# Both directions of a chunked state-space core in one masked matrix a head, with dt folded into its rows

## The chip, the cores and the metric

The kernel runs on one core of a Trainium2 chip. The metric is device time in microseconds (us), the median of several executions. Engines are named as the profile names them: PE is TensorE (matmuls), PEld its weight loads, DVE is VectorE, ACT is ScalarE, POOL is GpSimd, SP is SyncE, which here only starts transfers (DMA).

## What is computed

The program is one step through two layers of a hybrid backbone over 128 context and 512 latent tokens: four parallel mixers, a gated sum, an output projection, and an MLP. The change is inside one mixer, the bidirectional state-space mixer (SSD, 8 heads of 64 channels, 2 groups of 64 states, chunks of 128 tokens). Per direction and chunk the reference computes

```
acum = cumsum(dt * (-exp(a_log)))
lmat = exp(where(lower, acum_t - acum_s, -1e30))
xdt = x * dt
scores = einsum('thn,shn->tsh', C, B) * lmat
y_diag = einsum('tsh,shp->thp', scores, xdt)
decay_end = exp(acum_last - acum)
chunk_states = einsum('shn,shp->hpn', B * decay_end, xdt)
y_off = einsum('thn,hpn->thp', C, s_start) * exp(acum)
```

and the mixer's output is `y_f + flip(y_b) + d_skip * x`, where the backward direction runs on flipped inputs. All of this is fp32.

## The kernel before

**Tiling.** Tokens lie in five chunks of 128 (one of context, four of latents). The sequence of the work is a hand-written plan: each mixer is a generator, and a string of letters says which generator advances next (`c` is one chunk of the SSD core, `l` the S5 output product, `g` a gate product, `p`/`P` the projections of the attention). A list scheduler then places the instructions on each engine's queue; each engine works its queue strictly in order. The large products split fp32 weights into a high and a low part: ACT casts the high part (`wh`, L214), DVE or POOL subtracts for the low part (`wl`, L198), and PE multiplies three times (L225, L226, L227). PE works on these products between all the small matmuls of the core.

**The core** is `ssd_core`. It runs once in each layer, over chunks `c`, and inside over two groups `g` of four heads. Matrices have the source token in the partitions and the target token in the columns. For a chunk:

- two PE matmuls of B against C (L1006), and four DVE multiplications by a triangle (L1008) make `cm`, the masked scores, [128, direction, group, 128] (tile `scb`);
- POOL multiplies x by dt for each direction (L1020, recorded at the helper's line L1015): two tiles `sxd`, 128x512;
- for a group, two transfers bring the cumulated decay of the four heads to all partitions (L1029, tiles `sseg`), ACT saves a column (L1030), DVE and POOL subtract (L1031), DVE takes the minimum of the two directions (L1035), ACT exponentiates (L1036). One tile `ee` serves both directions, since each uses its own triangle;
- DVE makes the weights `wd` of the state (L1038), POOL multiplies `ee` by the backward mask into `mf` (L1042), DVE multiplies `ee` by the forward mask (L1043);
- PE makes, for each head, two matmuls into one PSUM region: `ee` by forward `xd` (L1046) and `mf` by backward `xd` (L1047);
- after both groups POOL makes `sxw` twice and `sxD` once (L1048, L1049, recorded at L1015), DVE adds `sxD` to the products in place of x (L1050), PE makes the chunk's states (L1054), ACT copies them out (L1058).

**Buffers.** `scb`, `sxd`, `sxw`, `sxD` and several tiles of other steps share one ring `tx` of 4 buffers; the `sseg` tiles share a ring `td` of 5. A write to a ring's buffer waits until all readers of the tile that held it are done. That orders, for one, POOL's `sxd` of a chunk behind the state matmuls of the chunk before.

## Time and profile before

| what | us |
|---|---|
| median of 3 executions | 3042.03 (3039.22 to 3045.7) |
| the profiled execution | 3031.18 |
| its span, first to last instruction | 3029.4 |
| PE busy | 2841.5 (94%) |
| DVE busy | 1724.3 (57%) |
| ACT busy | 1180.8 (39%) |
| POOL busy | 970.2 (32%) |
| mean granted clock of PE | 0.972 |

Busy is the share of the span in which an engine works on an instruction; waiting instructions are not in it. A granted clock of 1 is 2.4 GHz, 0.5 is 1.2 GHz, the only two levels; a mean between says how long each was held. The core of layer 0 lies between 455 and 575 us of the span, that of layer 1 between 1940 and 2075 us. Everything else in these stretches is products of other steps.

### The profile page before, as it was taken

The page shows a single profiled execution, that of the slowest core. Times are in us where ns is not written, and L with a number is a line of the kernel's source. Part 1 is how long each engine was busy: PE and PEld are TensorE (multiplying, and loading weights), DVE is VectorE, ACT ScalarE, POOL GpSimd, SP SyncE. Part 2 cuts the span into 40 slices and gives each one's busy share as a digit, 9 for nine tenths or more (in the row PEclk, how much of TensorE's full clock was granted, in tenths as well). Part 3 has the DMA queues.
Part 4 walks back from the last instruction along what each step waited for, and adds up shares of the span by engine and source line. Part 5 has one row for each costly group of instructions (what it writes and reads, how often), then busy time and mean ns, then how long its engine had stood idle before and what let it go on. Part 6 is the DMA issues. An engine that isn't in the chain of part 4 may idle for free.

```text
span 3029.4 us, 54102 instructions
## 1 busy us (share of the span) xinstructions
PE 2841.5 (94%) x20782; PEld 2663.8 (88%) x20782; DVE 1724.3 (57%) x3730; ACT 1180.8 (39%) x2660; POOL 970.2 (32%) x1057
## 2 busy tenths in 40 slices
PE   7888898999899999999999889999999999999999
PEld 5888788898689888899998879888898999999999
DVE  7859847765643456646235686475666436433333
ACT  4343463343344242323234536523535434322322
POOL 3737506523212222424111670264131122211111
PEclk9989999999899999999999999999999999999999
DMA  6752253224432735434444323431252323222222
GB/s 238 239 180 90 71 152 111 81 90 134 145 109 72 239 102 174 146 115 154 153 146 132 121 82 111 140 107 58 91 181 86 110 87 112 63 77 74 74 77 84
DMA packets 241858, 364.21 MB, mean 120 GB/s; under 512 B 42272, under 2 KB 104480, under 8 KB 241600
## 3 DMA queue, kind: packets, MB, share of 16 engines
q1 hardware_dynamic: 226848, 336.97, 35.5%
q10 hardware_dynamic: 14752, 23.78, 2.1%
q8 instruction: 164, 2.69, 0.4%
q14 instruction: 94, 0.77, 0.1%
HBM read 294.98 MB, written 65.68 MB: 119 GB/s over the span
## 4 chain that ended last, share of the span: by engine, by line
PE 71%; DVE 15%; issue 4%; DMA 3%; ACT 3%; POOL 2%; SPq 0%; ACTq 0%; DVEq 0%; POOLq 0%
PE dn L225 20%; PE dn L226 19%; PE dn L227 19%; DVE wl L198 2%; DVE B L767 2%; PE mx L290 1%; PE mx L1287 1%; PE pb L1331 1%; PE mx L1461 1%; PE mx L1325 1%; PE mx L1416 1%; DMA sseg<-acum 1%; DVE sc L764 1%; DVE sc L765 1%; PE mx L745 1%
## 5 line engine op out<-in xcount | busy, mean ns | idle before, releaser
L198 POOL TENSOR_TENSOR wl<-wr,wh 128x512 fp32r<-128x512 f32 x207 | 282.6, 1366 | 1271.2 <-ACT wh L214 1151.3
L214 ACT CAST wh<-wr 128x512 fp32r<-128x512 f32 (+1 forms) x614 | 377.4, 620 | 612.9 <-PE dn L226 539.6
L198 DVE TENSOR_TENSOR wl<-wr,wh 128x512 fp32r<-128x512 f32 (+1 forms) x407 | 325.7, 804 | 304.7 <-ACT wh L214 297.3
L225 PE MATMUL dn<-hh,wh 128*128 128x320 f32 x1328 | 422.6, 319 | 8.4 <-ACT us L697 2.7
L227 PE MATMUL dn<-hh,wl 128*128 128x320 f32 x1328 | 420.2, 317 | 3.4 <-DVE wl L198 3.4
L226 PE MATMUL dn<-hl,wh 128*128 128x320 f32 x1328 | 420.1, 316 | 2.8 <-DVE hl L403 1.5
L225 PE MATMUL dn<-nh,wh 128*128 128x320 f32 x992 | 311.7, 315 | 6.6 <-DVE r L1755 6.6
L225 PE MATMUL dn<-fh,wh 128*128 128x320 f32 x1008 | 313.6, 311 | 2.0 <-DVE s5u L595 1.3
L226 PE MATMUL dn<-nl,wh 128*128 128x320 f32 x992 | 308.9, 312 | 3.9 <-DVE nl L403 1.6
L227 PE MATMUL dn<-fh,wl 128*128 128x320 f32 x1008 | 312.0, 310 | 0.0
L226 PE MATMUL dn<-fl,wh 128*128 128x320 f32 x1008 | 311.8, 309 | 0.0
L227 PE MATMUL dn<-nh,wl 128*128 128x320 f32 x992 | 308.0, 311 | 0.0
L226 PE MATMUL dn<-wl,hh 128*128 128x256 f32 (+1 forms) x880 | 258.2, 294 | 16.3 <-DVE wl L198 14.2
L225 PEld LDWEIGHTS dn<-hh,wh 128*128 128x128 f32 x1328 | 254.3, 192 | 16.5 <-issue 3.1
L225 PE MATMUL dn<-wh,hh 128*128 128x256 f32 (+1 forms) x880 | 259.7, 297 | 8.5 <-DVE dtraw L1216 4.2
L227 PEld LDWEIGHTS dn<-hh,wl 128*128 128x128 f32 x1328 | 254.2, 191 | 8.9 <-DVE wl L198 4.6
L226 PEld LDWEIGHTS dn<-hl,wh 128*128 128x128 f32 x1328 | 254.2, 191 | 7.1 <-POOL hl L198 2.1
L227 PE MATMUL dn<-wh,hl 128*128 128x256 f32 (+1 forms) x880 | 257.1, 293 | 0.0
L1547 DVE SCALAR_TENSOR_TENSOR x<-dn,mod,x 128x192 f32<-128x192 f32 (+2 forms) x240 | 98.0, 437 | 225.2 <-PE dn L227 222.2
L225 PE MATMUL dn<-B,wh 128*128 128x320 f32 x640 | 207.8, 326 | 15.1 <-ACT B L834 4.4
L226 PE MATMUL dn<-B,wh 128*128 128x320 f32 x640 | 203.4, 318 | 0.0
L227 PE MATMUL dn<-B,wl 128*128 128x320 f32 x640 | 201.3, 315 | 0.0
(400 smaller groups left out, 6715.0 us busy)
## 6 DMA issues: line engine op xcount, KB each, us to landing
wr<-in_w_fc_dram SPq DMA_DIRECT2D x256, 256.0 KB, 2.8
wa<-in_w_mod_dram SPq DMA_DIRECT2D x160, 256.0 KB, 4.5
wr<-in_w_gate_dram SPq DMA_DIRECT2D x128, 256.0 KB, 2.8
wr<-in_w_tok_dram SPq DMA_DIRECT2D x80, 256.0 KB, 2.9
wr<-in_w_branch_dram SPq DMA_DIRECT2D x64, 256.0 KB, 3.0
acc<-gth SPq DMA_DIRECT2D x48, 320.0 KB, 3.0
gold<-acc SPq DMA_DIRECT2D x48, 320.0 KB, 3.3
gate<-gah ACTq DMA_DIRECT2D x70, 160.0 KB, 2.0
```

The source lines that it names most:

```text
L198: engine.tensor_tensor(out=out, in0=full, in1=hi, op=ALU.subtract)
L214: nc.scalar.copy(out=hi, in_=raw)
L225: nc.tensor.matmul(ps, sh, vh, start=first, stop=False)
L226: nc.tensor.matmul(ps, sh, vl, start=False, stop=False)
L227: nc.tensor.matmul(ps, sl, vh, start=False, stop=last)
L290: nc.tensor.matmul(acc[r0:r0 + 32, i * 256:i * 256 + 256], cpad[:, k, :], raw(part, k // 2)[:, c0:c0 + 256], start=(n_ < 4), stop=(n_ >= 4),)
L745: nc.tensor.matmul(xs[:, ri, g * NI:(g + 1) * NI], pm[:, ri, g * 128:(g + 1) * 128], U[:, g0 + g], start=True, stop=True)
L764: ve.tensor_tensor(out=pair[:, 0], in0=src, in1=re.to_broadcast(shp), op=ALU.mult)
L765: ve.tensor_tensor(out=pair[:, 1], in0=src[:, :, ::-1], in1=im.to_broadcast(shp), op=ALU.mult)
L767: ve.tensor_tensor(out=dst, in0=dst, in1=pair[:, i], op=ALU.add)
L1287: nc.tensor.matmul(sc[:, n, c0:c0 + (k1 - k0) * 128], qT[rows[n], g, ct], kT[rows[n], k0:k1].rearrange("p k c -> p (k c)"), start=True, st ...
L1547: nc.vector.scalar_tensor_tensor(out=xs, in0=ps[:, c0:c1], scalar=mods[l][:, part * 8 + f, s:s + 1], in1=xs, op0=ALU.mult, op1=ALU.add)
```

## The change

dt moves out of x and into the rows of the masked scores. For each head, `md = cm_forward * dt_forward + cm_backward * dt_backward`, with dt as one number per partition (the source token), is made by one ACT copy with a scale and one DVE multiply-add, both 128x128 (tile `smd`, ring `tx`). One DVE multiplication `ee * md` replaces the two by `cm`, and one PE matmul per head, with x itself as the moving side, replaces two. The two `sxd` tiles and `mf` are gone. The states (`sxw`) and `sxD` are as before.

```
-            xd = [times(dt[:, c, 8 * d:8 * d + 8], "sxd") for d in range(2)]
             out2 = mx()
...
+                md = tx([128, 4, 128], "smd")
+                for h in range(4):
+                    n = 4 * g + h
+                    nc.scalar.activation(out=md[:, h], in_=cm[:, 0, g], func=AF.Copy, scale=dt[:, c, n:n + 1])
+                    nc.vector.scalar_tensor_tensor(
+                        out=md[:, h], in0=cm[:, 1, g], scalar=dt[:, c, 8 + n:9 + n], in1=md[:, h], op0=ALU.mult,
+                        op1=ALU.add,
+                    )
                 sg = [td([128, 4, 128], "sseg") for _ in range(2)]
...
-                eng("mf").tensor_tensor(out=mf, in0=ee, in1=cm[:, 1, g].unsqueeze(1).to_broadcast(b4), op=ALU.mult)
-                eng("ef").tensor_tensor(out=ee, in0=ee, in1=cm[:, 0, g].unsqueeze(1).to_broadcast(b4), op=ALU.mult)
+                nc.vector.tensor_tensor(out=ee, in0=ee, in1=md, op=ALU.mult)
                 for h in range(4):
                     hc = slice((4 * g + h) * 64, (4 * g + h) * 64 + 64)
-                    nc.tensor.matmul(yp[:, hc], ee[:, h], xd[0][:, hc], start=True, stop=False)
-                    nc.tensor.matmul(yp[:, hc], mf[:, h], xd[1][:, hc], start=False, stop=True)
+                    nc.tensor.matmul(yp[:, hc], ee[:, h], r["xs"][:, c, hc], start=True, stop=True)
```

Below the change the new lines are L1030 (ACT) and L1031 (DVE) for `smd`, L1050 for the one multiplication, L1053 for the one matmul; the old L1030, L1031, L1035, L1036 become L1038, L1039, L1043, L1044, and L1054 and L1058 become L1060 and L1064. Over the program 80 matmuls leave PE, 40 instructions leave POOL, 80 come to ACT and 80 to DVE. Outside of the two cores and the work just behind them the queues stand as before, but for a few neighbours that change places.

PE, first chunk of layer 0, the products of both groups, before:

```order
L1046 MATMUL mx_4724<-sxd_4720,sseg_4726 128x64
L1047 MATMUL mx_4724<-sxd_4722,sseg_4727 128x64
L225 MATMUL dn_5869<-B_5397,wh_5826 128x320
L226 MATMUL dn_5869<-B_5397,wh_5826 128x320
L227 MATMUL dn_5869<-B_5397,wl_5827 128x320
L225 MATMUL dn_5869<-B_5397,wh_5826 128x320
L1046 MATMUL mx_4724<-sxd_4720,sseg_4748 128x64
L1047 MATMUL mx_4724<-sxd_4722,sseg_4749 128x64
```

and now (the first two rows are the first group, the next two the second):

```order
L1053 MATMUL mx_4720<-xs_3580,sseg_4731 128x64 x4
L1053 MATMUL mx_4720<-xs_3580,sseg_4757 128x64 x4
L225 MATMUL dn_5889<-B_5417,wh_5846 128x320
L226 MATMUL dn_5889<-B_5417,wh_5846 128x320
L227 MATMUL dn_5889<-B_5417,wl_5847 128x320
L225 MATMUL dn_5889<-B_5417,wh_5846 128x320
```

Eight matmuls a group became four, and the four matmuls of another product that stood between the groups stand behind them.

ACT, second chunk of layer 0, around the copy of the first chunk's states (`d`), with the engines whose work each row waits for, before:

```order
L214 CAST wh_6012<-wr_6010 128x512 [waits PE_49]
L1036 ACTIVATE sseg_5002<-sseg_5002 128x512 [waits DVE_49,Activation_49]
L1030 COPY dcl_4708<-sseg_5025 128x4 [waits DMAHW4_49]
L859 CAST B_5422<-yf_5898 128x320 [waits DVE_49]
L1030 COPY dcl_4708<-sseg_5073 128x4 [waits DMAHW5_49]
L851 ACTIVATE sg_5940<-dn_5915,bgluh_5675 128x320 [waits PE_49,Pool_49]
L1058 COPY d_947_4709<-mx_4724 128x512 [waits DVE_49,PE_49]
L1036 ACTIVATE sseg_5024<-sseg_5024 128x512 [waits DVE_49,Activation_49]
```

and now:

```order
L214 CAST wh_6032<-wr_6030 128x512 [waits PE_49]
L1038 COPY dcl_4708<-sseg_5086 128x4 [waits DMAHW4_49]
L859 CAST B_5442<-yf_5918 128x320 [waits DVE_49]
L1038 COPY dcl_4708<-sseg_5087 128x4 [waits DMAHW5_49]
L1030 ACTIVATE smd_5028<-scb_4991,dtd_4678 128x128 [waits DMAHW6_49,PE_49]
L1030 ACTIVATE smd_5028<-scb_4991,dtd_4678 128x128 x3
L1064 COPY d_947_4709<-mx_4720 128x512 [waits PE_49]
L851 ACTIVATE sg_5960<-dn_5935,bgluh_5695 128x320 [waits PE_49,Pool_49]
```

The four copies of the second group's `smd` wait for PE (the state matmuls of the chunk before free the ring's buffer) and stand ahead of the copy of the states. The same stands at eight of the 20 groups, four in each layer.

DVE, second chunk of layer 0, first group, from the minimum (L1035) to the multiplication (L1043), with the engines waited for, before:

```order
L1035 TENSOR_TENSOR sseg_5002<-sseg_5002,sseg_5003 128x512 [waits Pool_49]
L854 SCALAR_TENSOR_TENSOR yf_5898<-dn_5869,bglu_5673,sg_5895 128x320 [waits DVE_49,PE_49]
L198 TENSOR_TENSOR wl_6013<-wr_6010,wh_6012 128x512 [waits Activation_49]
L1050 TENSOR_TENSOR xs_3580<-mx_4724,sxD_4774 128x512 [waits Pool_49]
L1038 TENSOR_TENSOR swd_5001<-sseg_5002,dtd_4678 128x4 [waits Activation_49]
L1038 TENSOR_TENSOR swd_5001<-sseg_5002,dtd_4678 128x4
L198 TENSOR_TENSOR B_5422<-yf_5898,B_5422 128x320 [waits Activation_49]
L1008 TENSOR_TENSOR scb_4987<-pa_4992,triu 128x128 [waits PE_49]
L1008 TENSOR_TENSOR scb_4987<-pa_4992,tril 128x128
L1031 TENSOR_TENSOR sseg_5073<-sseg_5073,dac_4687 128x512 [waits DMAHW5_49,Activation_49]
L852 TENSOR_SCALAR sg_5940<-sg_5940 128x320 [waits Activation_49]
L1043 TENSOR_TENSOR sseg_5002<-sseg_5002,scb_4987 128x512 [waits DVE_49,Pool_49]
```

and now (L1043 is the minimum, L1050 the multiplication):

```order
L1043 TENSOR_TENSOR sseg_5011<-sseg_5011,sseg_5012 128x512 [waits Pool_49]
L1008 TENSOR_TENSOR scb_4991<-pa_4996,triu 128x128 [waits PE_49]
L1008 TENSOR_TENSOR scb_4991<-pa_4996,tril 128x128
L1031 SCALAR_TENSOR_TENSOR smd_5002<-scb_4991,dtd_4678,smd_5002 128x128 [waits Activation_49] x3
L854 SCALAR_TENSOR_TENSOR yf_5918<-dn_5889,bglu_5693,sg_5915 128x320 [waits PE_49]
L1031 SCALAR_TENSOR_TENSOR smd_5002<-scb_4991,dtd_4678,smd_5002 128x128 [waits Activation_49]
L1046 TENSOR_TENSOR swd_5001<-sseg_5011,dtd_4678 128x4 [waits Activation_49]
L1046 TENSOR_TENSOR swd_5001<-sseg_5011,dtd_4678 128x4
L198 TENSOR_TENSOR wl_6033<-wr_6030,wh_6032 128x512 [waits Activation_49]
L1039 TENSOR_TENSOR sseg_5086<-sseg_5086,dac_4687 128x512 [waits DMAHW4_49,Activation_49]
L1050 TENSOR_TENSOR sseg_5011<-sseg_5011,smd_5002 128x512 [waits DVE_49]
```

Between the minimum and the multiplication stand now four multiply-adds, each behind a wait for its ACT copy; `wl`, the low part of a weight, stands behind them.

## Rows read from the trace of the kernel before

**Rows 1.** The page's first part: busy us (share of the span) xinstructions.

```profile
PE 2841.5 (94%) x20782; PEld 2663.8 (88%) x20782; DVE 1724.3 (57%) x3730; ACT 1180.8 (39%) x2660; POOL 970.2 (32%) x1057
```

**Rows 2.** The page's chain that ended last, shares of the span by engine.

```profile
PE 71%; DVE 15%; issue 4%; DMA 3%; ACT 3%; POOL 2%; SPq 0%; ACTq 0%; DVEq 0%; POOLq 0%
```

**Rows 3.** Busy time by stretch, the two cores: length, busy (xinstructions), granted clock.

```profile
core 0: us, PE busy (x) PEld busy (x) DVE busy (x) ACT busy (x) POOL busy (x), PEclk, DMA share, GB/s
455.00:575.00 120.00, 110.31 (x729) 98.81 (x727) 89.70 (x158) 38.14 (x92) 72.55 (x62) 0.93 0.33 96
1940.00:2075.00 135.00, 120.31 (x809) 109.05 (x809) 94.32 (x150) 39.46 (x95) 79.89 (x67) 0.90 0.37 105
```

**Rows 4.** The same stretches, instructions that touch `sxd` alone (L1046, L1047 on PE).

```profile
core 0: us, PE busy (x) PEld busy (x) POOL busy (x), PEclk, DMA share, GB/s
455.00:575.00 120.00, 21.77 (x160) 20.83 (x160) 12.03 (x10) 0.93 0.33 96
1940.00:2075.00 135.00, 24.75 (x160) 23.80 (x160) 12.34 (x10) 0.90 0.37 105
```

**Rows 5.** PE in order of time: start, us, instruction, idle before and releaser.

```profile
480.21 0.41 PE L1046 MATMUL mx<-sxd,sseg 128*128 128x64 f32 x2 [1.74 <-DVE sseg L1043]
480.45 0.39 PE L1047 MATMUL mx<-sxd,sseg 128*128 128x64 f32 x2
480.67 0.39 PE L1046 MATMUL mx<-sxd,sseg 128*128 128x64 f32 x2
...
485.07 0.63 PE L1046 MATMUL mx<-sxd,sseg 128*128 128x64 f32 x2
485.50 0.64 PE L1047 MATMUL mx<-sxd,sseg 128*128 128x64 f32 x2
...
1962.93 0.47 PE L225 MATMUL dn<-wh,hh 128*128 128x256 f32 x1 [2.90 <-ACT wh L214]
1964.84 0.66 PE L1046 MATMUL mx<-sxd,sseg 128*128 128x64 f32 x2 [1.44 <-DVE sseg L1043]
```

**Rows 6.** Waits of PE in 440:600 and in 1930:2075: total us, times, longest.

```profile
PE mx L1046 <- DVE sseg L1043: 3.9, 3, 1.7
...
PE mx L1046 <- DVE sseg L1043: 6.5, 5, 2.4
...
PE dn L227 <- DVE wl L198: 1.1, 1, 1.1
```

**Rows 7.** Groups of instructions, whole run: busy us, mean ns | idle before, releaser.

```profile
L1042 POOL TENSOR_TENSOR sseg<-sseg,scb 128x512 f32<-128x512 f32 x20 | 28.7, 1436 | 20.8 <-ACT sseg L1036 14.9 <-ACT dcl L1030 4.5 <-DVE qss L1195 1.4
L1043 DVE TENSOR_TENSOR sseg<-sseg,scb 128x512 f32<-128x512 f32 x20 | 25.3, 1271 | 0.3 <-POOL sseg L1042 0.3
L1015 POOL TENSOR_TENSOR sxd<-xs,dtd 128x512 f32<-128x512 f32 x20 | 24.4, 1223 | 2.2 <-PE mx L1054 2.2
L1031 DVE TENSOR_TENSOR sseg<-sseg,dac 128x512 f32<-128x512 f32 x20 | 21.7, 1085 | 13.3 <-ACT dcl L1030 9.3 <-PE dn L226 3.9
```

**Rows 8.** Single lines on DVE: duration ns min/median/max, first and last start, forms.

```profile
L1043 DVE TENSOR_TENSOR sseg<-sseg,scb x20: 674/1524/1776, 478.5 to 2045.5; 128x512 f32<-128x512 f32 x20
L1050 DVE TENSOR_TENSOR xs<-mx,sxD x10: 675/684/694, 490.3 to 2049.9; 128x512 f32<-128x512 f32 x10
L1187 DVE TENSOR_TENSOR qks<-qkn,rtab x112: 209/279/1389, 130.0 to 2220.9; 128x128 f32<-128x128 f32 x96, 128x64 f32<-128x64 f32 x16
L1141 DVE SCALAR_TENSOR_TENSOR B<-pa,sgn,B x40: 337/350/352, 665.6 to 2188.4; 128x128 fp32r<-128x128 f32 x40
```

**Rows 9.** Single lines on ACT, the same columns.

```profile
L1030 ACT COPY dcl<-sseg x40: 179/197/199, 468.8 to 2035.3; 128x4 f32<-128x4 f32 x40
L1036 ACT ACTIVATE sseg<-sseg x20: 623/632/634, 473.7 to 2040.6; 128x512 f32<-128x512 f32 x20
L1140 ACT ACTIVATE B<-pa,sgn x40: 362/368/374, 665.2 to 2188.0; 128x128 fp32r<-128x128 f32 x40
```

**Rows 10.** Waits, whole run: who waited for whom, total us, times, longest.

```profile
ACT dcl L1030 <- DMA sseg<-acum: 65.5, 30, 9.2
```

More of the change, by code (lines that the diff above doesn't have):

```diff
@@ L49 @@
 ENG = dict(
-    sub0="v", sub1="p", mf="p", ef="v", xd="p", xw="p", xD="p", off="p", z="v", qkn="p", qka="p", qkc="v",
+    sub0="v", sub1="p", xw="p", xD="p", off="p", z="v", qkn="p", qka="p", qkc="v",
     merge="p", diff="v", ctx="p", mn="v",
```

## The prediction

> **What bounds the kernel now.** The first view is the busy time of the engines: PE is busy 94% of the span, DVE 57%, the others less [rows 1]. The chain of work that ended last lies 71% on PE [rows 2]. So a microsecond of PE work that goes is worth up to a microsecond, if PE has other work ready. The question is whether that holds inside the two cores, so the second view is the busy time of the two stretches that contain them [rows 3]. PE is busy 110.3 of 120 us and 120.3 of 135 us: it stands idle 9.7 and 14.7 us, 24.4 us of 255 together. No other engine is near that: DVE is at 75% and 70%, POOL at 60% and 59%, ACT at 32% and 29%. The third view is what PE waits for there: the DVE multiplication L1043, whose result PE uses as weights, 3.9 us in three waits and 6.5 us in five, 10.4 us in all [rows 6]. Less than half of PE's idle time hangs on the core, and PE mostly has products of other steps between the core's matmuls. The clock costs something too: 0.93 and 0.90 are means, so of 120 and 135 us a loss of 8.4 and 13.5 us of PE work at full speed [rows 3]. The engine had stood idle 1.74, and 2.90 and 1.44 us, just before matmuls at the low level appear [rows 5].
>
> **PE, the matmuls that go.** A matmul of the core is two instructions (fp32). At the full clock the next starts 0.22 us later (480.45 to 480.67), at 1.2 GHz 0.43 us later [rows 5]. There are 160 of them in all, 320 instructions; the view of the stretches gives them 21.8 and 24.8 us, together 46.5 us, weight loads alongside [rows 4]. Half go: 46.5 / 2 = 23.3 us. With all of them at the full clock it would be 80 x 0.22 = 17.6 us, and that is the lower bound; the value taken is 23.3, because the idle times ahead of the slow ones come from the start of each core, which the change leaves. The matmul that stays has the same shape, so nothing is added on PE.
>
> **POOL, 40 instructions that go.** Twenty `mf` of 1.44 us and twenty `sxd` of 1.22 us, 28.7 + 24.4 = 53.1 us [rows 7]. POOL holds 2% of the chain that ended last [rows 2], so this is worth nothing by itself. But it frees DVE: the same DVE multiplication L1043 takes 0.67 us at best and 1.52 us in the median, while L1050, of the same size with one operand in PSUM, never takes over 0.69 us [rows 8]. The stretched ones run beside POOL.
>
> **DVE.** The multiplication stays, one for one: at best 20 x (1.27 - 0.67) = 12 us fall away, at worst none [rows 7, 8]. The subtraction L1031, at 1.09 us in the mean, has as much stretch to lose, about 20 x 0.41 = 8 us against the same 0.67. New are 80 multiply-adds, 128x128. No such instruction with all operands in SBUF is in the trace; the nearest are L1187, a two-tensor product of that shape, 0.21 at best, 0.28 in the median, and L1141, a multiply-add with one operand in PSUM, 0.35 [rows 8]. That is 16.7 to 28 us; I take 0.28, 22.3 us, since the operands are as in L1187. Net, DVE gains between 2 us (22 - 20) and 28 us of work in 255 us in which it now has 71 us free [rows 3]. It lies beside PE's work, except where it stands ahead of a wait of PE (below).
>
> **ACT.** New are 80 scaled copies, 128x128 from SBUF. A 128x4 copy takes 0.20, a 128x512 exponential 0.63 us; in proportion 0.30 us. The same shape from PSUM takes 0.37 [rows 9]. So 24 to 29 us, on an engine that is busy 78 of 255 us [rows 3]. ACT in the core mostly waits: 65.5 us for the transfers into `sseg` [rows 10]. It is covered too, but those waits stand in one queue with the new copies, and a weight cast (`wh`, L214) that stands behind is what PE's products wait for.
>
> **The new link in the chain.** Before, POOL's `sxd` waited for the ring's buffer, 2.2 us in the whole run [rows 7], and went straight to PE, beside the chain of `sseg`. Now eight of the 20 groups have four ACT copies that wait for the state matmuls of the chunk before, then the DVE multiply-add, and only then the multiplication that PE waits for. From the release to PE that was one `sxd`, 1.22 us; it is 4 x 0.30 + 0.28 + 0.67 = 2.15 us, 0.9 us more, 7 us over eight groups if PE has nothing else, zero if the `sseg` chain is later anyway. Behind the waiting copies stand the copy of the states, the next exponential, a gate's activation and a weight cast. Against this, the eight waits of PE for L1043 [rows 6] follow a multiplication that was stretched by up to 0.85 us; with 53 of the 152 us of POOL work in the two stretches gone [rows 3, 7], about half of it, 0.4 us each, 3 to 4 us. I take the cost whole, 7, and the relief as 4: net +3 us of waiting, between -10.4 (all of those waits go) and +7.
>
> **The rest at nothing.** The second `sseg` tile is free after the minimum, not after the matmuls, so transfers could start earlier; but the other tile of the pair still gates the ring of five, and SP's queue is in order. The clock: zero, with 10 us either way, about the loss of one stretch.
>
> The sum is -23.3 + 3 = -20.3 us. The profiled execution took 3031.2 us, so 3010.9 in its terms; it stands 10.8 us below the median of the three, 3042.0. Against the median I forecast **3021.7 us**, 0.7% less. What a measurement of this kernel can tell from no change is about 0.2%, 6 us.
>
> **Rivals.**
>
> (a) *The freed time turns into waits.* If the stretch is paced by the chain transfer, subtraction, minimum, exponential, multiplication through in-order queues, PE just waits 20 us longer. For it: ACT waits 65.5 us for the transfers [rows 10], and DVE holds a fair share of the chain [rows 2]. Against it: PE is 90% busy there with only 10.4 us of waits for the core [rows 3, 6], and in 12 of the 20 groups the new tile does not wait for PE. Time: 3042, give or take 5. Chance 0.16.
>
> (b) *The handshake between ACT and DVE holds the queues: slower.* The multiply-adds stand right ahead of other work on DVE, among it `wl` (L198), for which PE's products wait, and each waits for its ACT copy, which may stand behind an ACT wait for a transfer. If each of the 20 groups holds DVE, and PE behind it, for its four copies and four multiply-adds, that is 20 x (1.2 + 1.1) = 46 us against 23.3 saved: +23 us, 3065 us. It decides from the point at which more than half of each group's 2.3 us shows up as PE waiting. For it: the order of the queue. Against: PE waits for `wl` 1.1 us in the second core now [rows 6], and DVE has 71 us free. Chance 0.12.
>
> (c) *DVE, freed of POOL, lets PE run through.* Then the 10.4 us of waits go as well [rows 6], and with them part of the low clock, say half of the loss in one stretch, 5 to 8 us [rows 3]: -23.3 - 10.4 - 7 = -41 us, 3001. Chance 0.10.
>
> On (c) and (b) the Trainium skill has a rule, "SBUF — State Buffer", section "Who interferes with whom": a VectorE instruction with two SBUF inputs and a GpSimd instruction that reads SBUF cannot run together; the second to start is blocked for the whole of the first. The trace agrees as far as it goes: L1043, two SBUF inputs, stretches from 0.67 to 1.52 us, L1050 with one in PSUM does not [rows 8]. By the rule the change wins on 40 POOL instructions, but it also brings 80 short DVE instructions with two SBUF inputs, each of which can stand behind a whole POOL instruction; the 1.39 us maximum of L1187 against its 0.21 [rows 8] may be such a case. If one in each group did, 20 x 1.1 = 22 us of the relief on DVE would be eaten up, which makes (c) unlikelier than (b); the sum above stands without it.
>
> That the change does not do what it says is hardly open: the queue of PE shows one matmul a head where there were two.
>
> **How the numbers follow.** Forecast, a gain of 6 to 32 us, 0.62; (a) 0.16; (b) 0.12; (c) 0.10. Faster is 0.62 + 0.10 = 0.72, same 0.16, slower 0.12. The bounds of the sum are -23.3 - 10.4 - 7 = -41 and -17.6 + 7 + 10 = -1. The range goes from 3003 (half of (c) left out) to 3044 (most of (a) in): about 0.80.
>
> **What would show it.** In the profile after: one line of matmuls with about 23 us on PE where two had 46.5; PE's busy time lower by as much; POOL lower by some 53 us; the multiplication L1050 (new number) in the mean below 1.27 us; the new lines near 0.30 us on ACT and 0.28 us on DVE. PE's waits for the multiplication in the two stretches at 7 to 18 us. The prediction is wrong by (a) or (b) if PE's idle time in the stretches grows by over 15 us, and in (b) with waits on `wl`, `wh` or the `smd` lines.

## The result, and the profile after

The changed kernel takes **3007.8 us** in the median of four runs (3004.3 to 3010.8), the kernel before 3040.6 us in the same comparison: a ratio of 0.9889 with a 95% interval of 0.9872 to 0.9906, or 33 us less. The forecast was 3021.7 us, 20.3 us less, with a range of 3003 to 3044: faster, as forecast, and inside the range, but by 33 us where 20.3 were forecast. That is just past the 6 to 32 us of the forecast's main case, and nearer to rival (c) with its 3001 us.

The page after, busy time and chain, against [rows 1, 2]:

```profile
PE 2826.7 (94%) x20622; PEld 2647.7 (88%) x20622; DVE 1736.2 (58%) x3810; ACT 1203.0 (40%) x2740; POOL 919.4 (31%) x1017
PE 70%; DVE 17%; DMA 4%; issue 4%; ACT 2%; POOL 2%; SPq 1%; DVEq 0%; ACTq 0%; POOLq 0%
```

PE and POOL lost busy time (15 and 51 us), DVE and ACT gained (12 and 22 us). The shares hardly move; the gain has to be read in the two cores. Windows with the same clock times would hold different work, so from here on a stretch runs from one unchanged matmul to another, the same two in every kernel: one stretch for the core of layer 0, one for that of layer 1. First the kernel before, then the changed one (length, busy time of each engine, granted clock):

```profile
core 0: us, PE busy (x) PEld busy (x) DVE busy (x) ACT busy (x) POOL busy (x), PEclk, DMA share, GB/s
445.14:609.20 164.06, 149.98 (x1023) 137.13 (x1022) 113.52 (x203) 54.25 (x130) 91.58 (x80) 0.94 0.33 100
1951.54:2096.34 144.80, 130.11 (x895) 119.53 (x893) 103.88 (x173) 43.29 (x106) 86.85 (x76) 0.91 0.33 97
```

```profile
449.41:599.22 149.81, 135.35 (x943) 122.57 (x942) 118.49 (x243) 65.68 (x170) 69.71 (x60) 0.97 0.36 109
1941.67:2074.69 133.02, 119.21 (x814) 107.85 (x813) 104.09 (x206) 51.04 (x138) 64.43 (x58) 0.92 0.35 105
```

The two stretches together: 308.9 us before, 282.8 after, 26.0 less. PE's busy time is 25.5 of it (280.1 to 254.6); what is left, PE's idle time, is 28.8 before and 28.3 after. Between the stretches the kernels take the same (1342.3 and 1342.5 us), ahead of the first the changed kernel lost 4.3 us in unchanged code. The two profiled executions differ by only 20.4 us (3031.2 and 3010.8): the one of before ran 9 us under its median, the other 3 us over. Where those 12 us lie can't be read from single traces. Outside of the two stretches the same work takes 2720.5 us before, 2726.2 after, and between 2719 and 2730 in every kernel below but e5. PE's busy time is 10.7 us longer there after than before, which is why the page shows it lower by 15 us and not by 25.5. So a gain of 26.0 us can be read in the stretches; that it is 26 of the median's 33 is not shown.

The instructions of the core in the changed kernel, which answer to [rows 4, 7, 8, 9] (busy us, mean ns | idle time before them and its releasers), and two of them as single lines (shortest/median/longest ns):

```profile
L1053 PE MATMUL mx<-xs,sseg 128*128 128x64 f32 x160 | 24.0, 301 | 9.2 <-DVE sseg L1050 5.9 <-DVE swd L1046 1.7 <-DVE ry L188 1.4
L1031 DVE SCALAR_TENSOR_TENSOR smd<-scb,dtd,smd 128x128 f32<-128x128 f32 x80 | 38.2, 526 | 5.4 <-ACT smd L1030 5.4
L1030 ACT ACTIVATE smd<-scb,dtd 128x128 f32<-128x128 f32 x80 | 25.7, 391 | 7.0 <-DVE xs L1056 5.1 <-PE mx L1060 1.6 <-DVE scb L1008 0.2
L1050 DVE TENSOR_TENSOR sseg<-sseg,smd 128x512 f32<-128x512 f32 x20 | 19.4, 972 | 0.2
L1043 DVE TENSOR_TENSOR sseg<-sseg,sseg 128x512 f32<-128x512 f32 x20 | 16.0, 807 | 0.9 <-POOL sseg L1039 0.9
```

```profile
L1031 DVE SCALAR_TENSOR_TENSOR smd<-scb,dtd,smd x80: 335/344/1132, 468.4 to 2020.3; 128x128 f32<-128x128 f32 x80
L1050 DVE TENSOR_TENSOR sseg<-sseg,smd x20: 675/692/1754, 480.2 to 2021.8; 128x512 f32<-128x512 f32 x20
```

The matmuls L1053 alone, in the two stretches (length, busy time on PE and of their weight loads):

```profile
449.41:599.22 149.81, 10.95 (x80) 10.59 (x80) 0.97 0.36 109
1941.67:2074.69 133.02, 13.02 (x80) 11.95 (x80) 0.92 0.35 105
```

They fell from 46.5 us [rows 4] to 24.0, 22.5 us for a forecast of 23.3. The multiplication (now L1050) has a median of 0.69 us where it had 1.52 [rows 8]; the minimum (now L1043) has a mean of 0.81 us. Of the waits that answer to [rows 6, 10], and the two of the new instructions (total us, times, longest):

```profile
ACT dcl L1038 <- DMA sseg<-acum: 36.8, 26, 6.7
...
PE mx L1053 <- DVE sseg L1050: 5.9, 6, 2.2
DVE smd L1031 <- ACT smd L1030: 5.4, 5, 2.4
ACT smd L1030 <- DVE xs L1056: 5.1, 4, 1.8
```

PE waits for the multiplication 5.9 us, before 10.4, and ACT for the transfers 36.8, before 65.5. ACT's copies are as priced (25.7 us, forecast 24 to 29). DVE's multiply-adds are not: 38.2 us for a forecast of 16.7 to 28. Why, the timeline of the changed kernel shows, DVE and POOL alone, first four multiply-adds beside POOL, then four with POOL idle:

```profile
1966.38 3.49 DVE L1031 SCALAR_TENSOR_TENSOR smd<-scb,dtd,smd 128x128 f32<-128x128 f32 x4
...
1966.56 1.07 POOL L1015 TENSOR_TENSOR sxw<-xs,swd 128x512 f32<-128x512 f32 x1 [3.78 <-DVE swd L1046]
...
1967.60 1.08 POOL L1039 TENSOR_TENSOR sseg<-sseg,dac 128x512 f32<-128x512 f32 x1
...
1968.64 1.09 POOL L1015 TENSOR_TENSOR sxw<-xs,swd 128x512 f32<-128x512 f32 x1
```

```profile
1978.38 1.13 DVE L1031 SCALAR_TENSOR_TENSOR smd<-scb,dtd,smd 128x128 f32<-128x128 f32 x4
```

Alone, four take 1.13 us, 0.28 each, the price taken. Beside three POOL instructions in a row (two products and a subtraction) they take 3.49 us, and those three 3.24. The three start 1.04 us apart, and the shortest L1039 on POOL in this trace takes 1.04 us: POOL lost nothing here, DVE did the waiting. Over the whole trace, 21 of the 80 multiply-adds take over 1.25 times the shortest, and all 21 overlap a POOL tensor instruction; of the other 59, seven do.

### The profile page after: what moved, and what is told of

Same layout as the page of the kernel before. It is cut to its first block, busy times and chain, and to the rows that moved or that the text cites. A ratio compares the mean times of both kernels' runs of the same rounds, so it can differ in the third digit from the quotient of the medians.

```text
span 3009.0 us, 53906 instructions
## 1 busy us (share of the span) xinstructions
PE 2826.7 (94%) x20622; PEld 2647.7 (88%) x20622; DVE 1736.2 (58%) x3810; ACT 1203.0 (40%) x2740; POOL 919.4 (31%) x1017
## 3 DMA queue, kind: packets, MB, share of 16 engines
q1 hardware_dynamic: 226848, 336.97, 35.6%
## 4 chain that ended last, share of the span: by engine, by line
PE 70%; DVE 17%; DMA 4%; issue 4%; ACT 2%; POOL 2%; SPq 1%; DVEq 0%; ACTq 0%; POOLq 0%
PE dn L225 20%; PE dn L226 19%; PE dn L227 19%; DVE wl L198 2%; DVE B L767 2%; PE mx L290 2%; PE mx L1293 1%; PE pb L1337 1%; PE mx L1467 1%; PE mx L1331 1%; DVE sc L765 1%; DVE sc L764 1%; PE mx L1422 1%; DVE smd L1031 1%; DVE s5u L595 1%
## 5 line engine op out<-in xcount | busy, mean ns | idle before, releaser
L225 PEld LDWEIGHTS dn<-hh,wh 128*128 128x128 f32 x1328 | 257.8, 194 | 18.5 <-ACT us L697 4.2
L225 PE MATMUL dn<-B,wh 128*128 128x320 f32 x640 | 205.7, 322 | 17.6 <-DVE gth L1532 6.2
L225 PEld LDWEIGHTS dn<-nh,wh 128*128 128x128 f32 x992 | 187.8, 190 | 13.7 <-DVE r L1761 7.4
```

Of the source, the lines that this page charges most:

```text
L225: nc.tensor.matmul(ps, sh, vh, start=first, stop=False)
```

## Experiments

Each kernel was timed in five rounds beside the kernel before on the same chip. "Against before" is against the median of before in that comparison (3041.4 to 3042.7 us); the series ran on three chips, so two kernels are compared by this column. The intervals of the ratios are about ±0.15%, so a difference between two of these kernels under some 6 us says nothing. The stretches come from one trace each: two executions of the same kernel, the changed one and e1, differ by 2.2 us in the stretches and by 2.4 us in PE's idle time. Stretches, PE busy and PE idle are the sums over the two stretches above, from the same two matmuls in each trace.

| kernel | median us | ratio to before, 95% interval | against before | stretches | PE busy | PE idle |
|---|---|---|---|---|---|---|
| before | 3041 to 3043 | | | 308.9 | 280.1 | 28.8 |
| changed, again (e1) | 3009.8 | 0.9899 (0.9884 to 0.9914) | -32.0 | 285.0 | 254.4 | 30.7 |
| matmuls put back (e2) | 3043.0 | 1.0003 (0.9993 to 1.0012) | +1.2 | 311.6 | 277.3 | 34.3 |
| POOL put back, in the chain (e3) | 3034.3 | 0.9979 (0.9967 to 0.9991) | -7.5 | 307.0 | 264.7 | 42.2 |
| copies and multiply-adds doubled (e4) | 3015.8 | 0.9924 (0.9908 to 0.9940) | -26.0 | 293.0 | 257.4 | 35.6 |
| other ring (e5) | 3086.1 | 1.0158 (1.0138 to 1.0177) | +44.8 | | | |
| first subtraction on POOL (e6) | 3023.8 | 0.9942 (0.9923 to 0.9960) | -17.6 | 294.8 | 261.1 | 33.7 |
| mask product put back (e7) | 3024.3 | 0.9951 (0.9936 to 0.9966) | -17.1 | 295.4 | 255.6 | 39.8 |
| before, one matmul a head (e8) | 3015.6 | 0.9922 (0.9905 to 0.9938) | -25.8 | 290.3 | 255.5 | 34.9 |
| POOL put back, no reader (e9) | 3036.6 | 0.9983 (0.9972 to 0.9995) | -4.9 | 304.7 | 264.5 | 40.1 |
| second subtraction on DVE (e10) | 3007.6 | 0.9894 (0.9879 to 0.9910) | -33.9 | 278.9 | 253.3 | 25.6 |
| no copies, no multiply-adds (e11) | 3002.0 | 0.9871 (0.9857 to 0.9885) | -39.5 | 273.6 | 252.2 | 21.4 |
| POOL put back, in the tile of `sxD` (e12) | 3035.5 | 0.9980 (0.9968 to 0.9991) | -7.2 | 304.3 | 262.1 | 42.2 |

One thing limits all of these runs. The list scheduler places every edited kernel anew, so no run changes one thing alone. Take the instructions that two kernels have in common in the stretches: from before to e8, from e8 to e11, from e11 to e1, and from e1 to each of e2 to e12 without e5, 6 to 23% of PE's, 13 to 25% of ACT's and 20 to 36% of DVE's stand in another order. Between the changed kernel and e1, the same program, none do. What the order alone is worth was not measured; e5 (below) suggests that it can be much.

### The changed kernel again, and with the matmuls put back

e1 is the changed kernel itself. e2 adds, after each head's matmul, a second one of the same shape that adds zero:

```
-  nc.tensor.matmul(yp[:, hc], ee[:, h], r["xs"][:, c, hc], start=True, stop=True)
+  nc.tensor.matmul(yp[:, hc], ee[:, h], r["xs"][:, c, hc], start=True, stop=False)
+  nc.tensor.matmul(yp[:, hc], ee[:, h], zer, start=False, stop=True)
```

> The changed kernel again, as the measure for the runs beside it. Expected 28 to 38 us below the kernel before, as the first measurement.

> The changed kernel with the PE work of before: each head gets a second matmul of the same shape, with zeros as the moving side, so the result stays. POOL, DVE and ACT are as in the changed kernel. Theory A (23 us are the matmuls themselves, the other 10 come from DVE and POOL no longer stretching each other): 8 to 14 us below the kernel before. Theory B (all is PE: fewer matmuls also bring the clock and the waits): within 5 us of the kernel before. Theory C (the relief of DVE is most of it): over 20 us below it.

The whole gain went: 33.2 us more than the changed kernel, the time of before within 0.1%. The stretches of e2:

```profile
447.78:613.00 165.22, 146.93 (x1024) 135.99 (x1023) 118.73 (x243) 66.53 (x170) 70.78 (x60) 0.94 0.33 99
1956.89:2103.25 146.36, 130.39 (x895) 121.00 (x894) 102.42 (x206) 51.56 (x138) 64.93 (x58) 0.90 0.33 96
```

PE's busy time is up by 22.9 us against e1 and its idle time by 3.6, together 26.6 of the 33.2 us; the rest lies outside of the stretches, where the traces can't tell it from noise. This says what the matmuls are worth on top of the rest of the change. It also puts the rest, POOL's products out and the new instructions in, at nothing as long as PE makes two matmuls a head: +1.2 us against before. With one matmul a head the rest has to be measured from the other side.

### Before, with one matmul a head

e8 is the other side: the kernel before, without the second matmul; the POOL products stay.

```
-  nc.tensor.matmul(yp[:, hc], ee[:, h], xd[0][:, hc], start=True, stop=False)
-  nc.tensor.matmul(yp[:, hc], mf[:, h], xd[1][:, hc], start=False, stop=True)
+  nc.tensor.matmul(yp[:, hc], ee[:, h], xd[0][:, hc], start=True, stop=True)
```

> The kernel before with the second matmul of each head left out (its output lacks the other direction's part); the GpSimd products, both VectorE multiplications' waits and everything else stay as before. PE loses the same 160 instructions as by the change. Theory P, the gain is PE work and nothing else: 3010 to 3020 (22.5 us of matmuls, and some clock). Theory W, the chain through GpSimd and VectorE sets the pace, and the freed time on PE turns into waits for the multiplication: 3030 to 3042. Between the two, 3020 to 3030: part of it is given to the waits, and the removal of the GpSimd products is what lets the change keep it.

Measured 3015.6, in the band of "PE work and nothing else". The stretches are finer than that: PE's busy time fell by 24.6 us, its idle time rose by 6.1, more than the 2.4 us by which two executions of one kernel differ. A quarter of the freed time did turn into waits inside the cores.

### The rest of the change: POOL's work out, the new work in

e11 takes the new copies and multiply-adds out of the changed kernel, so that it differs from e8 by POOL's 40 products with what hangs on them (PE now reads x itself, the multiplication waits for no product, the ring holds fewer tiles) and from the changed kernel by the 160 new instructions and their tile.

```
-  md = tx([128, 4, 128], "smd")   (and the loop with the copy and the multiply-add)
-  nc.vector.tensor_tensor(out=ee, in0=ee, in1=md, op=ALU.mult)
+  nc.vector.tensor_tensor(out=ee, in0=ee, in1=cm[:, 0, g].unsqueeze(1).to_broadcast(b4), op=ALU.mult)
```

> The changed kernel without the 80 scaled copies and the 80 multiply-adds: the multiplication takes the mask of one direction alone, so the output lacks dt and the other direction. What it gains over the changed kernel is the price of the new instructions with their place in the chain. From the run with one matmul a head in the kernel before (25.8 us gained), the run with the mask product put back (14.5 us lost), and the gain of the change (32 us), the sum leaves 8 us for that price; the run that doubled them lost 6. Theory, the three add up: 2998 to 3006. Rival, the new instructions are hidden altogether and the doubling only hurt because it used a tile of the chain: 3006 to 3012. A second rival, VectorE is what holds the chain, and 38 us less on it bring more than 12: below 2998.

3002.0, within the first theory. So there is a path from before to the changed kernel with a measurement at each step: without the second matmuls 3015.6 (**-25.8 us**), without POOL's 40 products 3002.0 (**-13.7**), with the new instructions 3009.8 (**+7.5**), each step taken against the kernel before of its own comparison. The intervals of e11 and e1 only just meet, so the last step is at the edge of what can be told. By the stretches the same steps read -18.5, -16.8 and +11.5 us (to e1; +9.3 to the first trace of the changed kernel): the same signs, and sizes that hold to some 7 us. The stretches of e8 and e11:

```profile
448.25:605.31 157.06, 137.10 (x943) 125.00 (x942) 116.95 (x203) 54.14 (x130) 98.49 (x80) 0.95 0.35 104
1948.61:2081.88 133.27, 118.35 (x811) 107.90 (x810) 110.31 (x173) 42.33 (x106) 90.16 (x76) 0.91 0.35 106
```

```profile
447.52:597.83 150.31, 136.77 (x944) 125.24 (x943) 99.00 (x203) 54.93 (x130) 67.11 (x60) 0.94 0.36 109
1938.42:2061.66 123.24, 115.38 (x814) 105.57 (x813) 92.81 (x173) 42.91 (x106) 66.39 (x58) 0.93 0.39 114
```

From e8 to e11 DVE executes as many instructions (203 and 173), yet it is busy 35.5 us less. Take the shortest instruction of each kind (operation, tiles and shape) in the traces of all kernels but e5 as its price: in the stretches DVE's instructions last 96.7 us longer than that in e8, 94.4 us of it in instructions that overlap one of POOL's, and 58.6 us in e11, 55.6 of it beside POOL. So what went is the stretch beside POOL. PE's idle time falls from 34.9 to 21.4 us; its waits in e8, first and second stretch, then in e11:

```profile
PE dn L225 <- DVE yf L854: 6.2, 2, 4.0
PE mx L1046 <- DVE sseg L1043: 3.7, 4, 1.7
...
PE mx L1046 <- DVE sseg L1043: 5.3, 4, 2.2
...
PE mx L1045 <- DVE sseg L1042: 3.4, 2, 2.3
...
PE mx L1045 <- DVE sseg L1042: 2.2, 2, 1.8
```

The waits for the multiplication fall from 9.0 to 5.6 us, and the 6.2 us for `yf`, DVE work of another mixer, are gone: of the 13.5 us of idle time that went, only 3.4 hung on the core's own multiplication. From e11 to the changed kernel PE's idle time rises again, to 28.3 us in the first trace and 30.7 in e1.

### Doubling the new work

e4 computes the masked matrix a second time, into the free second `sseg` tile.

> The changed kernel with the new small work doubled: 80 more scaled copies on ACT and 80 more multiply-adds on DVE, into a tile that nobody reads, placed before the multiplication. Priced from the profile of the changed kernel that is 26 us on ACT and 27 to 38 us on DVE. If it is covered by PE's other work (as the sum of the prediction has it): at most 6 us slower than the changed kernel. If the handshake between ACT and DVE holds the queues (rival b): 20 to 46 us slower.

6.0 us more than e1, about what e11 says of the first set (7.5), though the intervals of e4 and e1 overlap. Neither is anything like the 46 us that rival (b) put on a handshake that holds the queues.

### POOL's work put back into the changed kernel, in four ways

e3 puts 40 products back ahead of the multiplication, half of which it must wait for; e7 only the 20 mask products that it waits for; e9 puts 40 products of x with dt behind the multiplication, with no reader; e12 repeats the product with the skip weights four times, in its own tile.

```
e3 +  nc.gpsimd.tensor_tensor(out=mf..., in0=xv, in1=dt..., op=ALU.mult)
e3 +  nc.gpsimd.tensor_tensor(out=mf, in0=ee, in1=cm[:, 1, g]..., op=ALU.mult)
e7 +  nc.gpsimd.tensor_tensor(out=mf, in0=ee, in1=cm[:, 1, g]..., op=ALU.mult)
      nc.vector.tensor_tensor(out=ee, in0=ee, in1=md, op=ALU.mult)
e9 +  for _ in range(2): nc.gpsimd.tensor_tensor(out=mf..., in0=xv, in1=dt..., op=ALU.mult)
      xD = times(dsk, "sxD")
e12 + for _ in range(4): nc.gpsimd.tensor_tensor(out=xD..., in0=xv, in1=dsk..., op=ALU.mult)
```

> The changed kernel with the 40 POOL instructions of before put back as dead work: per group one 128x512 product of x and dt and one of the exponential and the backward mask, both into a tile that nobody reads. Theory A: 8 to 14 us slower than the changed kernel, 20 to 25 below the kernel before. Theory B: within 5 us of the changed kernel. Theory C: over 20 us slower than the changed kernel.

> The changed kernel with 20 GpSimd instructions put back as dead work: the product of the exponential with one mask (1.44 us each in the kernel before), ahead of the VectorE multiplication, which overwrites what it reads and so waits for it, as it did before. The 20 products of x with dt stay out. The run with all 40 put back lost 24.5 us against the changed kernel (3034.3 against 3009.8); in it the multiplication that PE waits for stood behind both. Theory W, the loss comes from that wait, each microsecond of it ahead of PE costing about itself: the chain is 1.44 us longer instead of 2.7, so about half of the loss, 3020 to 3028. Theory S, the wait itself is harmless and only the x product ahead of it did it: 3008 to 3016. Theory T, any GpSimd product beside the multiplication does all of it: 3030 to 3036.

> The changed kernel with 40 GpSimd products of x with dt put back as dead work (about 49 us on that engine, nearly as much as the 40 that the change took out), placed after the multiplication, so that neither it nor PE waits for them; they write the second tile of the pair, which goes back to the ring a little later. Theory W, GpSimd work costs only where PE's operand stands behind it: within 6 us of the changed kernel, 3004 to 3016. Theory T, GpSimd's time itself stretches VectorE's instructions and delays what follows on GpSimd's queue (the products behind the state matmuls, the second subtraction): 3020 to 3035, as in the two runs that put back products ahead of the multiplication (3034.3 and 3024.3).

> The changed kernel with 40 GpSimd products put back as dead work, 48 us, none of which touches the chain: the product of x with the skip weights is computed five times over into its own tile, which the VectorE sum after the matmuls reads. In the run that put 40 products behind no reader (3036.6) they wrote the second tile of a segment pair, and the copies that wait for the transfers into that ring stood idle 53.2 us against 37.9. Theory R, that loss came from the tile, which goes back to the ring only after the products: without it 3006 to 3018. Theory T, GpSimd's time itself costs, by stretching VectorE's instructions and by holding its own queue: 3024 to 3040. Between them, 3018 to 3024: both.

After e3 (24.5 us over e1) the theory was that the wait of the multiplication does it, and e7 (14.9 us for half the products) fitted. e9 broke it: nobody waits for its products, and it costs 27.1 us. In its trace, the products and the multiply-adds, then the waits of the copies `dcl` in e9, e1 and e12:

```profile
L1052 POOL TENSOR_TENSOR sseg<-xs,dtd 128x512 f32<-128x512 f32 x40 | 49.4, 1242 | 20.2 <-DVE sseg L1043 19.8
L1031 DVE SCALAR_TENSOR_TENSOR smd<-scb,dtd,smd 128x128 f32<-128x128 f32 x80 | 47.1, 634 | 4.0 <-ACT smd L1030 4.0
...
ACT dcl L1038 <- DMA sseg<-acum: 53.2, 21, 6.9
...
ACT dcl L1038 <- DMA sseg<-acum: 37.9, 26, 6.0
...
ACT dcl L1038 <- DMA sseg<-acum: 57.6, 30, 6.1
```

The products start after the minimum, on whose tile they depend, and in 19 of the 20 groups they have ended when the multiplication starts. They run beside the multiply-adds ahead of it instead: 31 of the 80 take over 1.25 times the shortest, all beside POOL, where 21 did. And the copies `dcl` waited 53.2 us for transfers into the ring whose tile the products hold, where e1's waited 37.9. e12 takes the tile away as a cause, and the loss stays, 24.8 us; so does the wait of the copies, 57.6 us. So no single wait or tile explains it: forty products cost 24.5 to 27.1 us wherever they stand, some 0.6 to 0.7 us each, and e7's twenty 14.9. The stretches of e12, then its multiply-adds and its minimum, then the minimum in e1:

```profile
447.95:607.79 159.84, 138.88 (x943) 124.76 (x942) 119.11 (x243) 65.77 (x170) 92.52 (x80) 0.96 0.34 102
1953.44:2097.88 144.44, 123.25 (x815) 111.95 (x813) 111.67 (x206) 51.27 (x138) 88.10 (x79) 0.88 0.33 98
```

```profile
L1031 DVE SCALAR_TENSOR_TENSOR smd<-scb,dtd,smd 128x128 f32<-128x128 f32 x80 | 37.5, 514 | 6.5 <-ACT smd L1030 6.5
...
L1043 DVE TENSOR_TENSOR sseg<-sseg,sseg 128x512 f32<-128x512 f32 x20 | 22.6, 1140 | 7.8 <-POOL sseg L1039 7.8
```

```profile
L1043 DVE TENSOR_TENSOR sseg<-sseg,sseg 128x512 f32<-128x512 f32 x20 | 15.8, 795 | 1.3 <-POOL sseg L1039 1.3
```

POOL's own subtraction L1039 stands behind the products in its queue. So DVE's minimum waits for it 7.8 us instead of 1.3, and the minimum itself takes 1.14 us instead of 0.80. Nor are the products quite off the chain: DVE's sum (L1061) reads their tile, and PE's state matmuls (L1065) wait for the sum, 3.4 us where e1's waited 0.3:

```profile
PE mx L1065 <- DVE xs L1061: 3.4, 3, 1.6
```

By the measure used on e8 and e11, DVE's instructions are stretched by 79.0 us in e12 and by 73.6 in e1, only 5 us more. So in e12 most of the loss comes by way of what stands behind the products, and not by the stretch, which is 87.6 us in e9, 86.2 in e7 and 94.3 in e3. How much each way costs was not measured apart. PE ends up idle for 42.2 us instead of 30.7, and the same matmuls keep it busy 7.8 us longer, with the clock of the second stretch at 0.88 instead of 0.92.

Forty POOL products cost 13.7 us without the new DVE work (e8 to e11) and 24.5 to 27.1 us with it (e3, e9, e12). By the stretches it is 16.8 us against 19.3 to 22.0, so how much of that difference is real, and why, isn't settled. In e9 the multiply-adds are stretched further (47.1 us), in e12 they are not (37.5), so the multiply-adds alone don't explain it.

### Moving the subtractions, and another ring

e6 and e10 move one subtraction of each group, to POOL and to DVE; e5 takes the masked matrix from the ring `tw` instead of `tx`.

```
e6   -    sub0="v", sub1="p",     +    sub0="p", sub1="p",
e10  -    sub0="v", sub1="p",     +    sub0="v", sub1="v",
e5   -    md = tx([128, 4, 128], "smd")     +    md = tw([128, 4, 128], "smd")
```

> The changed kernel with the first of the two subtractions of each group on GpSimd too (20 instructions of 0.94 us less on VectorE, 20 of about 1.3 us more on GpSimd, one behind the other there). Theory W, what lies in the chain ahead of the multiplication sets what PE waits for: two subtractions in a row on one engine lengthen it by about 1 us a group, 10 to 20 us slower than the changed kernel: 3018 to 3030. Rival, VectorE, at 80% busy in the cores, is what holds the chain: 18.9 us less there bring 3 to 10 us: 3000 to 3007.

> The changed kernel with the second subtraction of each group on VectorE instead of GpSimd (20 of 1.3 us less there, 20 of 0.7 to 0.9 us more on VectorE), the mirror of the run that moved the first one to GpSimd and lost 14 us. Theory W, the length of the chain ahead of the multiplication decides: the two subtractions then stand one behind the other on VectorE, 1.4 us at best against 1.3 us side by side now, so nothing to gain, and VectorE has 18 us more: 3008 to 3020. Rival, GpSimd is what stretches the chain: 3 to 10 us faster, 3000 to 3007.

> The changed kernel with the masked matrix taken from another ring of buffers, so that the scaled copies no longer wait for the state matmuls of the chunk before. In the profile of the changed kernel the copies stand idle 5.1 us behind PE and 7.0 us behind the VectorE subtraction that uses the same ring. Theory: these waits are hidden, since PE has other work: 3006 to 3013. Rival, the new link in the chain costs what was forecast for it, up to 7 us: 3000 to 3005.

e6 loses 14.4 us against e1, as the theory had it: 20 more POOL instructions, 0.7 us each. That is the price found above, but here the two subtractions also stand in a row, so it may be the longer chain. e10 is 1.9 us below e1, between the bands of its theory and its rival, and their intervals overlap, so it isn't a better kernel as far as this measurement goes. Had 20 POOL instructions less brought 0.6 to 0.7 us each, it would have gained 12 to 14 us; what its 20 more DVE instructions took of that was not measured. Still, its stretches are the shortest of those that compute everything (278.9 us, PE idle 25.6), with POOL at its least.

e5, 76.8 us over e1, lies in neither of its bands and says nothing about the link that it was made for. Its expectation misreads the row: of the 7.0 us that the copies stand idle, 5.1 are behind DVE's sum and 1.6 behind PE. And `tw` is a ring that the S5 mixer beside the core lives on: with tiles taken from it, the order around the core came out so different that between the two matmuls that bound the first stretch (here 439.75 and 674.40 us) stand some 1140 PE instructions where the changed kernel has 943, and the stretches can't be compared. Another window around its first core:

```profile
core 0: us, PE busy (x) PEld busy (x) DVE busy (x) ACT busy (x) POOL busy (x), PEclk, DMA share, GB/s
416.42:654.73 238.31, 177.13 (x1026) 159.08 (x1025) 109.27 (x240) 95.31 (x206) 61.15 (x56) 0.72 0.33 92
```

PE is idle 61 us there and runs at a mean clock of 0.72. The wait on the ring was not tried in another way.

## Why the prediction was right, and where it was short

**PE.** 23.3 us forecast; 22.5 us of matmuls in the profile, 25.8 us of time when only the matmuls went (e8), 33.2 us when they came back on the changed kernel (e2); by the stretches 18.5 and 26.6. Right within what these runs can tell, and rival (a) falls: in e8, which leaves out the second matmuls alone, 6.1 us of 24.6 turned into idle time.

**POOL.** "This is worth nothing by itself" is the step that failed. It was argued from POOL's 2% of the chain, and the 3 to 4 us granted to DVE's relief came from the eight waits for L1043 alone. Measured, 13.7 us (e8 to e11), and 14.9 to 27.1 us when POOL work came back in (e3, e7, e9, e12). The chain credits a stretched DVE instruction to DVE, so POOL's share of it doesn't show what POOL costs. The relief also reaches all of DVE's instructions in the core, 35.5 us of busy time between e8 and e11, not only the one that PE waits for. That is the relief of rival (c), taken too small in the sum. Rival (c) as it was written did not come: of the 10.4 us of waits for the multiplication 5.9 are left, and PE's idle time fell by 0.5 us only. And the step failed with one matmul a head; with two, the rest of the change is worth +1.2 us (e2), close to the +3 of the sum. The two orders differ by 7 us, about as little as these runs can tell.

**The new instructions.** Forecast at +7 us of waiting; measured +7.5 (e11 to the changed kernel), +9.3 to +11.5 by the stretches. That the amount is right is in part luck. The reason given was the eight groups that wait for PE's state matmuls, and the copies stood idle for those 1.6 us in the whole run, and 5.1 us for the sum, which reads another tile of the ring. Whether any of that reached PE isn't shown, since e5 failed to try it. What can be seen is a cost on DVE that the forecast had too small: multiply-adds of 38.2 us where 22.3 were forecast. Alone they take the 0.28 us that was forecast, beside POOL up to 1.13.

**The Trainium skill's rule**, "SBUF — State Buffer", section "Who interferes with whom" (a VectorE instruction with two SBUF inputs and a GpSimd instruction that reads SBUF exclude each other), is borne out on DVE's side of the trace: at 1966 us each multiply-add beside POOL takes about as long as a POOL instruction, and all 21 long ones lie beside POOL. On POOL's side that stretch shows no delay. The prediction's estimate for the new instructions, one blocked in each of 20 groups, 22 us, stands against 21 long ones; they took 16 us more on DVE than forecast. The prediction named both sides of the rule and drew from it only that (c) is unlikelier than (b); the 40 products that went were the larger side.

**The clock.** Zero forecast, with 10 us either way. By the means shown, the loss is 22.9 us before (164.06 x 0.06 + 144.80 x 0.09) and 15.1 after: at most a gain of 8, inside the bound. The unchanged matmuls there kept PE busy for 233.6 us before (280.1 - 46.5) and 230.6 after (254.6 - 24.0), so only 3 us of it show as PE time. It is not added to the sum because it is part of what the runs measured for each step. One reading of [rows 5] was loose: behind the 1.74 us of idle time at 480.21 the next matmuls start 0.24 and 0.22 us apart, at the pace of the full clock.

**The sum.** -25.8 - 13.7 + 7.5 = -32.0, where -23.3 - 4 + 7 = -20.3 was forecast. The difference is POOL's term, 9.7 us, and 2.5 us on PE. The traces are kinder to the forecast: in the stretches PE's busy time is 25.5 us lower and its idle time 0.5 lower (e1: 25.7 lower and 1.9 higher), against -23.3 and +3 in the sum. Measured so, the sum missed by 3.5 to 5.7 us, and the other 7 to 8 us of the medians' gain lie where the traces can't show them.

**Rival (b)** falls with e4 (6 us for doubling what should have held the queues). The signs named for a wrong prediction didn't come: PE's idle time in the stretches is 0.5 us less than before. Of the signs for a right one, the matmuls (24.0 us), POOL's 51 us, the multiplication's mean of 0.97 us and ACT's 0.32 us a copy came; DVE's 0.48 us a multiply-add (0.28 named) and PE's 5.9 us of waits for the multiplication (7 to 18 named) did not.

## What to carry to other kernels

An engine that is off the chain is not free: price its instructions by what they stretch, from the shortest and the median time of the neighbour's instructions and from which of them overlap, and by what stands behind them in their own queue. Here forty POOL products cost 14 to 27 us, 0.3 to 0.7 us each, although POOL had 2% of the chain. To price a change of several parts, take them out one after the other on the chip, and in more than one order, since the parts need not add up. Look whether the queues kept their order around the edit; and compare traces between two unchanged instructions, not between two times.

## What the runs showed of the hardware

- Four multiply-adds of 128x128 with a scalar a partition take 1.13 us alone on DVE, 3.49 us beside three POOL instructions of 1.07 to 1.09 us, which themselves start 1.04 us apart and lose nothing (changed kernel, 1966 and 1978 us).
- Eighty scaled ACT copies of 128x128 last 0.39 us each but hold ACT for 25.7 us, 0.32 us each: they overlap (changed kernel).
- The same matmuls in the same stretches kept PE busy for 254.4 us (e1) and 262.1 us (e12): 7.8 us more for an engine that waited 11.5 us longer, with a mean clock of 0.88 instead of 0.92 in the second core. The total of idle time alone doesn't decide it: e7's PE was idle for 39.8 us and busy for 255.6, at 0.92 and 0.93.
